# Six and five row buffers for gathered experts, and the low part of the weights last

## The chip, the cores and the metric

The kernel runs on one core of a Trainium2 chip. The metric is the device time of one execution in microseconds (us). Three runs of the kernel before gave 5113.34, 5116.54 and 5140.52 us; the median, 5116.54 us, is the number that the change is measured against.

The core has five engines that run their own instruction queues: TensorE (PE in the profile, with its weight loads as PEld), VectorE (DVE), ScalarE (ACT), GpSimd (POOL) and SyncE (SP, which here only issues DMAs). Each engine takes its instructions strictly in the order in which they were written out, so an instruction that waits holds up everything behind it on its engine.

## The reference

Two layers of a transformer-like trunk over 512 latent tokens and 256 context tokens of width 1024, float32. A layer is a mixer part (attention, pooling and a short convolution from one input projection, gated and projected back) and then an expert part:

```python
q = (xc @ w_q).reshape(PEER_CHUNK, PEER_HEADS, 2, PEER_HALF)
s = jnp.einsum('thid,hikd->thik', q, sub_keys)
...                                     # top 16 of 256 candidates a head: eidx, gate
u = u_emb[eidx]
hid = jax.nn.gelu(jnp.einsum('td,thkd->thk', xc, u))
wgt = gate * hid
return jnp.einsum('thk,thkd->td', wgt, v_emb[eidx])
```

There are 16384 experts, 8 heads and 16 experts a head, so each token uses 128 experts: 128 rows of `u_emb` and 128 rows of `v_emb`, of 1024 floats each. Layer 1 treats the latent tokens alone.

## The kernel before, in words

The expert part is computed in two ways at once.

**Dense.** For most latent tokens (512 in layer 0, 384 in layer 1) the kernel computes the first product for all 16384 experts, `hid = uT x y`, multiplies by a gate matrix that is zero almost everywhere, and multiplies by all of `v`. Experts come in 32 groups `c` of four tiles `e` of 128 experts. `hidden` does the first product: per tile it loads `uraw` (512 KB, SP queue), splits it into a high part `uh` (ScalarE) and a low part `ul` (VectorE, `ul = uraw - uh`), and issues 24 matmuls, three for each of eight blocks `k` of the contraction: `uh*yh`, `uh*yl`, `ul*yh`. These three stand together in `mm3` (lines 98, 99, 100). `uh` and `ul` have two buffers each, `hid` three accumulators in PSUM. `values` does the second product in the same manner: two groups at a time, four quarters `dq` of the output width; per quarter it loads and splits two tiles `vraw` into `vh` and `vl` and issues 48 matmuls into two accumulators `dps`. `weigh` makes the other operand, `wh` and `wl`, from the stored or kept `hid` and the gates `G`.

**Gathered.** The 256 context tokens of layer 0 and the last 128 latent tokens of layer 1 use their 128 experts only. `gathered` works on 128 tokens at a time, one token to a partition: `fetch` (line 854) issues an indirect DMA on GpSimd that brings one expert's row for each of the 128 tokens (128x1024 floats, 512 KB) into a buffer named `row`, and one VectorE instruction uses it: line 868 for a row of `u` (multiply and sum) and line 878 for a row of `v` (multiply and add into `gacc`). That is 256 fetches for 128 tokens, 512 in layer 0 and 256 in layer 1. `row` has three buffers, so a fetch waits until VectorE is done with the row three before it.

**The order of the work.** The kernel is written in a tile framework that plans the order of every engine's instructions with its own timeline and priorities (`prio`). The gathered work has the lowest priority (`late`, 40000), so the planner puts its instructions where it thinks VectorE is free; the loads and splits of the dense weights come early (`-ahead`). The planned order is then fixed: the engines do not change it at run time.

In layer 0 the gathered rows run beside the rest of the mixer (weights `wraw`, split into `whi` and `wlo`, products `mm`), the routing (`keys`, `pick`, `gates`), `hidden` and most of `values`. In layer 1 they run beside the routing, `hidden` and `values`. There, `experts` stores the first 20 groups of `hid` and keeps the last 12 in memory, so that `hidden` and `values` of those 12 alternate; in that part `vh` and `vl` have `EC + 2 = 4` buffers each (line 1139), and four in the part that follows (line 1146).

Of the kernel before, what the change touches and what calls it, by code (L numbers as in the profile page):

```python
# [21 lines left out]
F32 = mybir.dt.float32  # L22
# [10 lines left out]
P = 128  # L33
D = 1024
KT = D // P
# [34 lines left out]
class Net:  # L70
# [695 lines left out]
    def hidden(self, l, y, up, uq, cs, ahead, keep=False):  # L766

        nc, a = self.nc, self.a
        tiles = []
        for c in cs:  # L770
            if l:
                ge = up.tile([P, 4, y.n], F32, name="ge", bufs=1 + self.EC)
                tiles.append(ge)
            for e in range(4):
                with self.prio(-ahead):
                    raw = up.tile([P, KT, P], F32, name="uraw", bufs=3)
                    nc.sync.dma_start(raw.rearrange("p k e -> p (k e)"), a["uT"][l, 4 * c + e])
                    uh = up.tile([P, KT, P], F32R, name="uh", bufs=2)
                    ul = up.tile([P, KT, P], F32R, name="ul", bufs=2)
                    self.split(uh, ul, raw)  # L780
                hid = uq.tile([P, y.n], F32, name="hid", bufs=3)
                for k in range(KT):
                    self.mm3(hid, uh[:, k], ul[:, k], y.h[:, k], y.l[:, k], k == 0, k == KT - 1)
                with self.prio(-ahead):
                    g = ge[:, e] if l else up.tile([P, y.n], F32, name="ge", bufs=4)
                    nc.scalar.activation(g, hid, AF.Gelu_apprx_tanh)
                    if not l:
                        nc.scalar.dma_start(self.hidd[c][:, e * y.n:(e + 1) * y.n], g)
            if l and not keep:
                with self.prio(-ahead):  # L790
                    nc.scalar.dma_start(self.hidd[c][:, :4 * y.n], ge.rearrange("p e t -> p (e t)"))
        return tiles
# [56 lines left out]
    def gathered(self, l, tiles, gp, gq, nat, late):  # L849

        nc, a = self.nc, self.a

        def fetch(t, idx, s):
            r = gp.tile([P, D], F32, tag="row", name="row", bufs=3)
            nc.gpsimd.indirect_dma_start(out=r, out_offset=None, in_=a[t],  # L855
                                         in_offset=bass.IndirectOffsetOnAxis(ap=idx[:, s:s + 1], axis=0))
            return r

        for row, idx, g, hsrc, i, dst in tiles:
            with self.prio(late):  # L860
                x = gp.tile([P, D], F32, name="gx", bufs=1)
                nc.sync.dma_start(x, nat[row:row + P, :])
                acc = gp.tile([P, D], F32, name="gacc", bufs=1)
                for h in range(8):
                    hid = gp.tile([P, 16], F32, name="ghid", bufs=2)
                    for k in range(16):
                        r = fetch("peer_u", idx, h * 16 + k)
                        nc.vector.scalar_tensor_tensor(out=r, in0=r, scalar=1.0, in1=x, op0=OP.mult, op1=OP.mult,  # L868
                                                       accum_out=hid[:, k:k + 1])
                    w = gp.tile([P, 16], F32, name="gw", bufs=2)  # L870
                    nc.scalar.activation(w, hid, AF.Gelu_apprx_tanh)
                    nc.vector.tensor_tensor(w, w, g[:, h * 16:h * 16 + 16], op=OP.mult)
                    for k in range(16):
                        r = fetch("peer_v", idx, h * 16 + k)
                        if h == 0 and k == 0:
                            nc.vector.tensor_scalar(acc, r, w[:, k:k + 1], None, op0=OP.mult)
                        else:
                            nc.vector.scalar_tensor_tensor(acc, r, w[:, k:k + 1], acc, op0=OP.mult, op1=OP.add)  # L878
            res = gp.tile([P, KT, P], F32, tag="row", name="gres", bufs=3)
            nc.sync.dma_start(res, hsrc.rearrange("(k p) t -> p k t", p=P))  # L880
            tr = gq.tile([P, 4, P], F32, tag="gtr", name="gtr", bufs=1)
            for k in range(KT):
                nc.tensor.transpose(tr[:, k % 4], acc[:, k * P:(k + 1) * P], self.ident)
                nc.vector.scalar_tensor_tensor(res[:, k], tr[:, k % 4], self.modT[l][:, 40 + k, i:i + 1], res[:, k], op0=OP.mult, op1=OP.add)
            nc.sync.dma_start(dst.rearrange("(k p) t -> p k t", p=P), res)
# [10 lines left out]
    def run(self):  # L896
        nc, tc, a = self.nc, self.tc, self.a
        dt = lambda name, shape=(D, NT): tc.dram_tile(list(shape), F32, name=name)
        L = range(DEPTH)
        self.pd, self.od, self.md = [[dt(f"{n}{l}") for l in L] for n in ("pd", "od", "md")]  # L900
        self.qd, self.kd = [[dt(f"{n}{l}", (NH, P, 2, NT)) for l in L] for n in ("qd", "kd")]
        self.ld = [dt(f"ld{l}", (NH, P, NT)) for l in L]
        self.vd = [dt(f"vd{l}", (2, NH, P, NT)) for l in L]
        self.hmid = [dt(f"hmid{l}") for l in L]
        self.hout = dt("hout")
        self.natd = [dt("natd0", (NC, D)), dt("natd1", (P, D))]
        self.gd = dt("gd", (NX // 32, P, P * 32))
        self.hidd = dt("hidd", (32, P, 4 * NX))
        self.EC, self.stored = 2, 20
        X, Cx = Stream(0, NX, 0), Stream(NX, NC, 1)  # L910
        with ExitStack() as root:
            self.consts(self.pool(root, "consts"))
            ges = eh = h = None
            for l in L:
                ges, eh, h = self.trunk(l, X, Cx, ges, eh, h)
                ges, eh, h = self.ffn(l, ges, eh, h)
            eh.close()
            ges.close()
# [205 lines left out]
    def experts(self, l, y, up, uq, eu, e2):  # L1124


        n, EC, S = y.n, self.EC, self.stored
        with ExitStack() as es:
            self.hidden(l, y, up, uq, range(S), 12000)
            acc = self.pool(es, f"acc{l}").tile([P, KT, n], F32, name="acc")  # L1130
            va, vq = self.pool(es, f"va{l}"), self.pool(es, f"vq{l}", 1, PSUM)
            with ExitStack() as ev:
                vb = self.pool(ev, f"vb{l}")
                for c in range(S, 32 + EC, EC):
                    if c < 32:
                        ge = self.hidden(l, y, up, uq, range(c, c + EC), 0, True)
                    if c > S:
                        cs = range(c - EC, c)
                        self.values(l, n, cs, self.weigh(l, n, va, cs, had), lambda dq: (vb, 3, vb, EC + 2), vq, acc, c == S + EC)
                    had = ge  # L1140
                eu.close()
                e2.close()
            vb = self.pool(es, f"vc{l}", side="right")
            for c in range(0, S, EC):
                cs = range(c, c + EC)
                self.values(l, n, cs, self.weigh(l, n, va, cs), lambda dq: (vb, 3, vb, EC + 2), vq, acc, False,
                            vb if c == S - EC else None)
# [73 lines left out]
```

## Time and profile before

| | |
|---|---|
| median of three runs | 5116.54 us |
| profiled execution | 5126.48 us, span 5124.7 us |
| TensorE, busy share of the span | 95% |
| VectorE | 77% |
| ScalarE | 39% |
| GpSimd | 23% |
| DMA, mean | 250 GB/s |
| mean granted TensorE clock | 0.975 of full speed |

Busy TensorE is not TensorE at its peak: consecutive matmuls overlap, so the time of one matmul in the tables (its latency) is longer than the step from one to the next. The step is better read from a stretch that holds only matmuls of one kind, as the stretch divided by their count. A wait is the idle time of an engine before an instruction, put down to whatever released it last.

### The profile page before, as it was taken

Reading aid. Unit: us, or ns where it says so; the run is one execution under the profiler, and the core shown is the slowest. Engines: PE = TensorE matmul, PEld = TensorE weight load, DVE = VectorE, ACT = ScalarE, POOL = GpSimd, SP = SyncE. Lnnn points to the kernel's source line nnn. Section 1 sums busy time; section 2 is a strip of 40 time slices with the busy share of each in tenths; the row PEclk is TensorE's granted clock in tenths of the full one; section 3 lists DMA queues with packets and bytes.
Section 4 is the critical chain, followed back from the end, with each engine's and each line's share of the span. In section 5 each row is a group of like instructions: output and inputs, shape, how many; then the busy total and the mean of one; then the engine's idle time right before and its main releaser. Section 6 shows DMA issues by size and latency. Waiting matters only on the chain.

```text
span 5124.7 us, 74008 instructions
## 1 busy us (share of the span) xinstructions
PE 4846.5 (95%) x27373; PEld 4187.1 (82%) x27373; DVE 3946.3 (77%) x7996; ACT 1984.5 (39%) x2970; POOL 1199.9 (23%) x1060
## 2 busy tenths in 40 slices
PE   8999999798799999989999999999999999899999
PEld 5689787576588788768888879888679889899999
DVE  5468785977799998568888766777459999787885
ACT  4346665222233344323222334555334344332333
POOL 0012000144433343243334100100000433244320
PEclk9999999899899999999999999999899999999999
DMA  8668554488888888999999734543355888988995
GB/s 308 239 201 237 179 169 129 145 271 276 281 302 270 297 300 323 323 315 320 342 335 337 261 114 161 175 135 118 120 169 173 282 297 329 319 313 292 335 330 177
DMA packets 509419, 1280.77 MB, mean 250 GB/s; under 512 B 42880, under 2 KB 225024, under 8 KB 500736
## 3 DMA queue, kind: packets, MB, share of 16 engines
q1 hardware_dynamic: 302816, 669.35, 38.7%
q0 software_dynamic: 132352, 449.90, 26.1%
q10 hardware_dynamic: 73888, 156.79, 8.2%
q8 instruction: 215, 3.52, 0.3%
q14 instruction: 148, 1.21, 0.1%
HBM read 1098.13 MB, written 177.73 MB: 249 GB/s over the span
## 4 chain that ended last, share of the span: by engine, by line
PE 47%; DMA 14%; issue 11%; DVE 9%; POOL 3%; ACT 1%; POOLq 0%; DVEq 0%; ACTq 0%; SPq 0%
DMA row<-peer_v,ix 8%; PE dps L100 6%; PE dps L99 6%; PE dps L98 6%; DMA row<-peer_u,ix 5%; PE mm L98 4%; PE mm L100 4%; PE mm L99 4%; PE hid L100 4%; PE hid L98 4%; PE hid L99 3%; POOL row L855 3%; DVE gacc L878 2%; PE gps L760 1%; PE qk L100 1%
## 5 line engine op out<-in xcount | busy, mean ns | idle before, releaser
L100 PE MATMUL hid<-yh,ul 128*128 128x512 f32 (+1 forms) x2048 | 760.8, 373 | 55.3 <-DVE ul L94 54.9
L855 POOL DMA_INDIRECT row<-peer_v,ix x384 | 586.7, 1528 | 876.9 <-DVE gacc L878 537.4
L98 PE MATMUL hid<-yh,uh 128*128 128x512 f32 (+1 forms) x2048 | 758.3, 371 | 21.0 <-ACT yh L286 13.1
L855 POOL DMA_INDIRECT row<-peer_u,ix x384 | 503.5, 1311 | 1113.7 <-DVE row L868 614.3
L99 PE MATMUL hid<-yl,uh 128*128 128x512 f32 (+1 forms) x2048 | 755.9, 369 | 3.6 <-DVE yl L287 3.6
L100 PE MATMUL dps<-wh,vl 128*128 128x512 f32 (+1 forms) x2048 | 740.9, 364 | 11.8 <-DVE vl L94 11.8
L99 PE MATMUL dps<-wl,vh 128*128 128x512 f32 (+1 forms) x2048 | 741.1, 364 | 7.0 <-DVE wl L94 7.0
L98 PE MATMUL dps<-wh,vh 128*128 128x512 f32 (+1 forms) x2048 | 735.3, 364 | 8.9 <-ACT vh L93 8.9
L98 PE MATMUL mm<-hi,whi 128*128 128x512 f32 (+1 forms) x1856 | 665.5, 359 | 19.6 <-ACT rg L481 6.0
L100 PE MATMUL mm<-hi,wlo 128*128 128x512 f32 (+1 forms) x1856 | 658.6, 357 | 25.3 <-DVE wlo L94 25.0
L99 PE MATMUL mm<-lo,whi 128*128 128x512 f32 (+1 forms) x1856 | 659.8, 356 | 1.7 <-DVE lo L94 1.7
L878 DVE SCALAR_TENSOR_TENSOR gacc<-row,gw,gacc 128x1024 f32<-128x1024 f32 x381 | 488.2, 1281 | 166.9 <-DMA row<-peer_v,ix 165.4
L868 DVE SCALAR_TENSOR_TENSOR row<-row,gx 128x1024 f32<-128x1024 f32 x384 | 466.9, 1222 | 168.5 <-DMA row<-peer_u,ix 167.9
L94 DVE TENSOR_TENSOR wlo<-wraw,whi 128x1024 fp32r<-128x1024 f32 (+1 forms) x356 | 428.1, 1204 | 178.5 <-ACT whi L93 175.7
L93 ACT ACTIVATE uh<-uraw 128x1024 fp32r<-128x1024 f32 x256 | 271.3, 1060 | 689.5 <-PE hid L99 657.4
L93 ACT ACTIVATE whi<-wraw 128x1024 fp32r<-128x1024 f32 (+1 forms) x356 | 369.9, 1043 | 385.3 <-PE mm L99 270.1
L93 ACT ACTIVATE vh<-vraw 128x1024 fp32r<-128x1024 f32 x256 | 270.1, 1057 | 633.6 <-PE dps L99 387.9
L100 PEld LDWEIGHTS hid<-yh,ul 128*128 128x128 f32 x2048 | 391.2, 191 | 107.4 <-DVE ul L94 69.3
L98 PEld LDWEIGHTS hid<-yh,uh 128*128 128x128 f32 x2048 | 392.1, 192 | 63.6 <-ACT yh L286 14.7
L100 PEld LDWEIGHTS dps<-wh,vl 128*128 128x128 f32 x2048 | 386.3, 189 | 53.2 <-DVE vl L94 12.7
L99 PEld LDWEIGHTS hid<-yl,uh 128*128 128x128 f32 x2048 | 391.4, 191 | 44.7 <-DVE yl L287 5.0
L98 PEld LDWEIGHTS dps<-wh,vh 128*128 128x128 f32 x2048 | 386.6, 189 | 49.9 <-ACT vh L93 9.7
(337 smaller groups left out, 9481.1 us busy)
## 6 DMA issues: line engine op xcount, KB each, us to landing
uraw<-uT SPq DMA_DIRECT2D x256, 512.0 KB
vraw<-v SPq DMA_DIRECT2D x256, 512.0 KB
wraw<-w_in SPq DMA_DIRECT2D x216, 512.0 KB
gd<-gst ACTq DMA_DIRECT2D x28, 2048.0 KB
mw<-w_mod SPq DMA_DIRECT2D x96, 512.0 KB
wraw<-wq SPq DMA_DIRECT2D x80, 512.0 KB
hidd<-ge ACTq DMA_DIRECT2D x128, 256.0 KB
G<-gd SPq DMA_DIRECT2D x32, 1024.0 KB
```

The source lines that it names most:

```text
L93: self.nc.scalar.activation(hi, src, AF.Copy)
L94: self.nc.vector.tensor_tensor(lo, src, hi.bitcast(F32), op=OP.subtract)
L98: mm(ps, lh, rh, start=start, stop=False)
L99: mm(ps, lh, rl, start=False, stop=False)
L100: mm(ps, ll, rh, start=False, stop=stop)
L760: nc.tensor.matmul(ps[:, t], A[:, a_, :, t_], B[x][:, a_, :, t_], start=x == 0, stop=x == 1)
L855: nc.gpsimd.indirect_dma_start(out=r, out_offset=None, in_=a[t], in_offset=bass.IndirectOffsetOnAxis(ap=idx[:, s:s + 1], axis=0))
L868: nc.vector.scalar_tensor_tensor(out=r, in0=r, scalar=1.0, in1=x, op0=OP.mult, op1=OP.mult, accum_out=hid[:, k:k + 1])
L878: nc.vector.scalar_tensor_tensor(acc, r, w[:, k:k + 1], acc, op0=OP.mult, op1=OP.add)
```

## The change

Three edits. The row buffers become six in layer 0 and five in layer 1 (they were three). In layer 1, `vh` and `vl` have three buffers instead of four while `hidden` and `values` alternate; a buffer of `vh` and one of `vl` together are as large as the two more row buffers. And a tile of `hidden` issues its 16 matmuls with the high part `uh` first and its 8 matmuls with the low part `ul` behind them.

```diff
@@ hidden
                 hid = uq.tile([P, y.n], F32, name="hid", bufs=3)
+                mm = nc.tensor.matmul
                 for k in range(KT):
-                    self.mm3(hid, uh[:, k], ul[:, k], y.h[:, k], y.l[:, k], k == 0, k == KT - 1)
+                    mm(hid, uh[:, k], y.h[:, k], start=k == 0, stop=False)
+                    mm(hid, uh[:, k], y.l[:, k], start=False, stop=False)
+                for k in range(KT):
+                    mm(hid, ul[:, k], y.h[:, k], start=False, stop=k == KT - 1)
@@ gathered
-            r = gp.tile([P, D], F32, tag="row", name="row", bufs=3)
+            r = gp.tile([P, D], F32, tag="row", name="row", bufs=self.rows[l])
...
-            res = gp.tile([P, KT, P], F32, tag="row", name="gres", bufs=3)
+            res = gp.tile([P, KT, P], F32, tag="row", name="gres", bufs=self.rows[l])
@@ run
-        self.EC, self.stored = 2, 20
+        self.EC, self.stored, self.rows = 2, 20, (6, 5)
@@ experts
-                        self.values(l, n, cs, self.weigh(l, n, va, cs, had), lambda dq: (vb, 3, vb, EC + 2), vq, acc, c == S + EC)
+                        self.values(l, n, cs, self.weigh(l, n, va, cs, had), lambda dq: (vb, 3, vb, EC + 1), vq, acc, c == S + EC)
```

In the changed kernel the lines behind `hidden` have a number four higher: 855, 868 and 878 become 859, 872 and 882; the three matmuls of `hidden` stand in lines 784, 785 and 787. The planner makes a new order from these edits. Three places of it follow.

TensorE, layer 0, from one tile of `hidden` to the next, before (line 98 is `uh*yh`, 99 `uh*yl`, 100 `ul*yh`; the number of a name tells its buffer's use):

```order
L98 MATMUL hid_21152<-yh_14901,uh_21148 128x512
L99 MATMUL hid_21152<-yl_14902,uh_21148 128x512
L100 MATMUL hid_21152<-yh_14901,ul_21149 128x512
L98 MATMUL hid_21186<-yh_14901,uh_21182 128x512
L99 MATMUL hid_21186<-yl_14902,uh_21182 128x512
```

and the same turn from tile to tile in the changed kernel:

```order
L784 MATMUL hid_22444<-yh_14901,uh_22440 128x512
L785 MATMUL hid_22444<-yl_14902,uh_22440 128x512
L787 MATMUL hid_22444<-yh_14901,ul_22441 128x512 x8
L784 MATMUL hid_22478<-yh_14901,uh_22474 128x512
L785 MATMUL hid_22478<-yl_14902,uh_22474 128x512
```

Before, the low part was read by every third matmul, first by the third one; now all eight matmuls that read it stand at the end of the tile, and the first of them is the 17th.

GpSimd at the start of the gathered work of layer 0, before (`z` is a buffer of the convolution, of which GpSimd clears the two edges; rows of `peer_u` and `peer_v` are fetched 16 at a time):

```order
L855 DMA row<-peer_u,ix_11017 128x1024 x12
L573 MEMSET z 128x1
L574 MEMSET z 128x1
L573 MEMSET z 128x1
L574 MEMSET z 128x1
L855 DMA row<-peer_u,ix_11017 128x1024 x4
L855 DMA row<-peer_v,ix_11017 128x1024 x3
```

and now:

```order
L859 DMA row<-peer_u,ix_11017 128x1024 x16
L859 DMA row<-peer_v,ix_11017 128x1024 x5
L573 MEMSET z 128x1
L574 MEMSET z 128x1
L573 MEMSET z 128x1
L574 MEMSET z 128x1
L859 DMA row<-peer_v,ix_11017 128x1024 x4
```

Twelve fetches stood ahead of the first two buffers `z`, now 21.

VectorE in layer 1, while the gate matrix is made (`gA`, `gB`, `gE`) beside `hidden`, before (`gacc` uses a row of `v`):

```order
L94 TENSOR_TENSOR ul<-uraw,uh 128x1024
L752 TENSOR_TENSOR gB_40070<-gE,sl_35872 128x1024
L750 TENSOR_TENSOR gA<-iota_38404,sl_35870 128x1024
L753 TENSOR_TENSOR gB_40071<-gE,sl_35873 128x1024
L751 TENSOR_TENSOR gE<-iota_38404,sl_35871 128x1024
L878 SCALAR_TENSOR_TENSOR gacc<-row,gw,gacc 128x1024
L94 TENSOR_TENSOR ul<-uraw,uh 128x1024
```

and in the changed kernel (line 872 uses a row of `u`):

```order
L94 TENSOR_TENSOR ul<-uraw,uh 128x1024
L872 SCALAR_TENSOR_TENSOR row,ghid<-row,gx 128x1024
L752 TENSOR_TENSOR gB_39842<-gE,sl_35872 128x1024
L753 TENSOR_TENSOR gB_39843<-gE,sl_35873 128x1024
L872 SCALAR_TENSOR_TENSOR row,ghid<-row,gx 128x1024
L750 TENSOR_TENSOR gA<-iota_38404,sl_35870 128x1024
L872 SCALAR_TENSOR_TENSOR row,ghid<-row,gx 128x1024
L752 TENSOR_TENSOR gB_39870<-gE,sl_35872 128x1024
L753 TENSOR_TENSOR gB_39871<-gE,sl_35873 128x1024
L872 SCALAR_TENSOR_TENSOR row,ghid<-row,gx 128x1024
L751 TENSOR_TENSOR gE<-iota_38404,sl_35871 128x1024
L94 TENSOR_TENSOR ul<-uraw,uh 128x1024
```

One gathered row stood between two splits `ul` here, now four do. Over a whole layer the gathered rows stand closer together: counted in VectorE's order, the last of layer 0's 512 rows had 118 splits `vl` ahead of it and has 65 now, and the last of layer 1's 256 rows had 245 and has 209.

## Rows read from the trace of the kernel before

**Rows 1.** The page: busy us, share of the span and instructions of each engine.

```profile
PE 4846.5 (95%) x27373; PEld 4187.1 (82%) x27373; DVE 3946.3 (77%) x7996; ACT 1984.5 (39%) x2970; POOL 1199.9 (23%) x1060
```

**Rows 2.** Two slices of `values` alone: length, busy (count) by engine, clock, DMA.

```profile
2562.40:2690.50 128.10, 127.31 (x562) 105.09 (x562) 111.37 (x149) 35.39 (x45) 47.08 (x36) 1.00 0.97 335
...
4868.50:4996.60 128.10, 128.10 (x742) 127.92 (x742) 113.46 (x169) 46.99 (x65) 32.61 (x22) 1.00 0.95 330
```

**Rows 3.** TensorE's waits on splits: total, times, longest, in us.

```profile
PE hid L100 <- DVE ul L94: 54.9, 33, 5.8
PE mm L100 <- DVE wlo L94: 28.9, 16, 4.2
...
PE dps L100 <- DVE vl L94: 11.8, 2, 11.0
...
PE dps L98 <- ACT vh L93: 8.9, 2, 7.1
...
PE dps L99 <- DVE wl L94: 7.0, 5, 3.4
```

**Rows 4.** Waits around the gathered rows: who waited for whom.

```profile
POOL row L855 <- DVE row L868: 743.8, 273, 14.3
POOL row L855 <- DVE gacc L878: 660.8, 271, 15.0
...
DVE row L868 <- DMA row<-peer_u,ix: 167.9, 105, 7.6
DVE gacc L878 <- DMA row<-peer_v,ix: 165.4, 97, 6.4
```

**Rows 5.** GpSimd in order of time, `hidden` of layer 0: start, length, what, idle before.

```profile
2235.98 0.93 POOL L855 DMA_INDIRECT row<-peer_v,ix  x1 [2.99 <-DVE row L868]
2238.55 1.67 POOL L855 DMA_INDIRECT row<-peer_v,ix  x1 [1.64 <-DVE gacc L878]
```

**Rows 6.** VectorE in the same stretch.

```profile
2241.73 1.28 DVE L878 SCALAR_TENSOR_TENSOR gacc<-row,gw,gacc 128x1024 f32<-128x1024 f32 x1 [1.12 <-DMA row<-peer_v,ix]
2242.93 1.22 DVE L94 TENSOR_TENSOR ul<-uraw,uh 128x1024 fp32r<-128x1024 f32 x1
2247.23 2.61 DVE L878 SCALAR_TENSOR_TENSOR gacc<-row,gw,gacc 128x1024 f32<-128x1024 f32 x2 [3.08 <-DMA row<-peer_v,ix]
```

**Rows 7.** The costliest groups: count, busy us, mean ns, idle before.

```profile
L878 DVE SCALAR_TENSOR_TENSOR gacc<-row,gw,gacc 128x1024 f32<-128x1024 f32 x381 | 488.2, 1281 | 166.9 <-DMA row<-peer_v,ix 165.4
L868 DVE SCALAR_TENSOR_TENSOR row<-row,gx 128x1024 f32<-128x1024 f32 x384 | 466.9, 1222 | 168.5 <-DMA row<-peer_u,ix 167.9
...
L93 ACT ACTIVATE vh<-vraw 128x1024 fp32r<-128x1024 f32 x256 | 270.1, 1057 | 633.6 <-PE dps L99 387.9
```

**Rows 8.** Slices of 10 us around TensorE's longest wait for `ul`.

```profile
4390.00:4400.00 10.00, 6.63 (x39) 6.31 (x37) 1.23 (x2) 2.50 (x3) 1.36 (x2) 1.00 0.94 365
4400.00:4410.00 10.00, 7.56 (x30) 7.56 (x31) 4.81 (x7) 1.06 (x1) 2.61 (x2) 0.66 0.81 264
```

**Rows 9.** The stretches with gathered rows, whole and three parts.

```profile
1025.00:2947.00 1922.00, 1821.65 (x8988) 1496.75 (x8987) 1580.94 (x2774) 606.82 (x843) 704.48 (x520) 0.98 0.88 303
3972.00:4997.00 1025.00, 969.10 (x5962) 945.83 (x5961) 882.01 (x1477) 373.90 (x559) 375.75 (x257) 0.98 0.88 312
1025.00:1409.00 384.00, 326.71 (x1388) 257.96 (x1387) 287.50 (x403) 104.86 (x133) 164.90 (x142) 0.94 0.81 276
2306.00:2819.00 513.00, 509.80 (x2233) 420.99 (x2234) 444.30 (x600) 148.13 (x189) 186.98 (x137) 0.99 0.96 333
4484.00:4997.00 513.00, 495.86 (x2818) 492.20 (x2817) 430.04 (x597) 171.76 (x236) 193.42 (x141) 0.99 0.91 318
```

**Rows 10.** DMA issues of `values` in layer 0: count, KB each.

```profile
vraw<-v SPq DMA_DIRECT2D x256, 512.0 KB
...
G<-gd SPq DMA_DIRECT2D x32, 1024.0 KB
gel<-hidd SPq DMA_DIRECT2D x32, 1024.0 KB
```

## The prediction

> **What bounds the kernel now.** I read the page's busy times first. TensorE is busy for 95% of the span and no other engine for more than 77% [rows 1], so the end can only move if TensorE's idle time moves. Then its step: in two slices that hold almost nothing but `values`, 562 matmuls of 512 columns take 128.1 us and 742 of 384 columns the same, so a matmul costs 0.228 us and 0.173 us [rows 2]. A tile of `hidden` (24 matmuls) is then 5.5 us in layer 0 and 4.15 us in layer 1, and none of the edits changes a matmul's count or form. What can be won is waits.
>
> The list of TensorE's waits names who it waits for [rows 3]. The largest is the one for `ul`: 54.9 us in 33 waits. With `wlo` (28.9), `vl` (11.8) and `wl` (7.0) TensorE spends 102.6 us waiting for splits by VectorE. Why is VectorE late? It is not full. But it stands still 333 us for gathered rows that have not landed (167.9 and 165.4) [rows 4], and as it keeps its order, a split behind such a row is late too. GpSimd is not the cause: its fetches wait 1405 us (743.8 + 660.8) for VectorE to give a row buffer back. So the loop is: buffer given back, fetch, landing, use, three rows deep.
>
> How deep must it be? One stretch of `hidden` shows it. The fetch issued at 2235.98 is read by VectorE at 2241.73, after a wait, 5.75 us later; the next, issued at 2238.55, is read at 2247.23, 8.7 us later [rows 5, 6]. In `hidden` of layer 0 about two rows stand to a `ul`, so three rows back is 1.5 tiles, 8.2 us at TensorE's pace: no reserve against 5.75 to 8.7.
>
> **The change part by part.**
>
> *Low part last.* It removes nothing; it lets `ul` come 14 matmuls later (17th instead of third). That is 14 x 0.228 = 3.2 us in layer 0 and 14 x 0.173 = 2.4 us in layer 1. The mean of the 33 waits is 54.9 / 33 = 1.7 us, under both; the longest, 5.8 us, is over [rows 3]. At most 54.9 / 2.4 = 22 waits could be as long as the delay, in truth few are; I leave 10 us standing and take -45. The ends are -55 and 0 (0 if VectorE falls behind by so much more that the new slack is used up). `uh` is given back after 16 matmuls instead of 23, so ScalarE's split for the tile after next starts earlier; `ul` is given back at the end as before, and its split (1.22 us [rows 6]) then has 16 matmuls more before it is due. What is late next is `uh` itself, but ScalarE is busy for 39% only [rows 1].
>
> *Six and five row buffers.* Six rows back is three tiles, 16 us in the stretch above, against 5.75 to 8.7. Counting in the order all VectorE work that stands between a row's release and its next use, at the mean times of [rows 7] and of each other group, the median of that work grows from 7.4 to 13.1 us, and of 762 uses those with less than 7.3 us (the middle of 5.75 and 8.7) fall from 371 to 25. So most of the 333 us of VectorE's stalls should go as long as a fetch takes no longer than now. TensorE is paid only where a split stands behind: `wlo`, `vl`, `wl`, 47.7 us [rows 3] (the `ul` part is counted above). The ends are 0 and -48. I take -25, half: the same order also puts rows closer together, so part of the lead is spent.
>
> The Trainium skill (DMA: Bandwidth & Descriptors, section Anatomy of one DMA — SWDGE path) puts a GpSimd transfer at about 2.0 us plus its bytes over 436 GB/s; for a row fetch of 512 KB that is an estimate of 3.2 us. By that, three buffers would do already, this term would be 0 and the sum -31 instead of -56. The trace disagrees: 5.75 and 8.7 us from issue to use.
>
> *The clock.* Before TensorE's longest wait for `ul` the granted clock was 1.00 (2.4 GHz), in the 10 us after it 0.66, a mix of both levels, the lower being 1.2 GHz [rows 8]. The two stretches with gathered rows run at 0.98 on the mean [rows 9]: 2% of 2947 us, 59 us, is the most that lower clocks can take there, and most of it stands beside idle time that is counted already. With fewer waits I take -6; the ends are -20 and 0.
>
> *Three instead of four buffers of `vh` and `vl`.* It holds for 6 rounds of 4 quarters in layer 1. In a quarter two tiles are held, so one instead of two can be split ahead; the second waits until the first of the running quarter is done, and then takes a ScalarE and a VectorE split, 1.06 [rows 7] and 1.22 us. If nothing hid that: 24 x 2.3 = 55 us. But TensorE's new order there works through both accumulators' share of the first tile before it turns to the second, which gives the first tile back at half the quarter (24 x 0.173 = 4.2 us before its end), and `hidden` tiles stand between rounds. With four buffers the wait for `vh` was 8.9 us in 2 waits [rows 3]. Ends 0 and +55; I take +5. If that cover is gone, it shows as waits of `dps` for `vh`.
>
> *Denser rows.* The same 512 rows of layer 0 now end 118 - 65 = 53 splits `vl` earlier, 53 x 24 x 0.228 = 290 us of TensorE's pace; layer 1's end 36 earlier, 36 x 24 x 0.173 = 149 us. VectorE's work is only moved. But bytes must come faster. Layer 0: 1922 us x 303 GB/s = 582 MB [rows 9], less what `values` moves in those 53 tiles (0.52 MB of `vraw` and a quarter of `G` and `gel`, 0.5 MB, each [rows 10]: 54 MB), so 528 MB in 1632 us, 324 GB/s. Layer 1: 1025 x 312 = 320 MB, less 36 x 0.9 = 32 MB (`G` and `gel` are three quarters as large with 384 tokens), 288 MB in 876 us, 329 GB/s. The DMA engines gave 333 GB/s over 513 us while TensorE kept its step (2233 x 0.228 = 509 us) [rows 9]. So it fits, barely: on the mean no loss, but where the planner packs most tightly, at the start of the gathered work in the mixer (21 fetches instead of 12 ahead of the first `z`), the rate asked for is over it. I take +15; ends 0 and +58 (below).
>
> **The sum.** -45 - 25 - 6 + 5 + 15 = -56 us on the profiled execution of 5126.5 us, 5070 us. That execution lay 10 us above the median of the runs, so the same -56 on 5116.5 us: **5060 us**, 1.1% faster.
>
> **The rivals.**
>
> *Slower: the DMA engines become the bound.* Place: both stretches of [rows 9]. The point from which it decides is the rate: under 324 GB/s in layer 0 or 329 in layer 1 the rows land later than the new order assumes, VectorE stands still at them as before, and the splits behind are late again. If the rate stays at the 318 GB/s of layer 1's second half, layer 0 needs 528 / 0.318 = 1660 us (+28) and layer 1 288 / 0.318 = 906 us (+30): +58, 5175 us. For it: with `hidden` in the mix no long stretch got over 318. Against: 333 in `values`, 365 in a 10 us slice [rows 8], and the 0.81 share and 276 GB/s of the mixer stretch, where fetches were limited by depth and not by the engines. The Trainium skill (DMA: Bandwidth & Descriptors, section SWDGE vs HWDGE vs iDMA) says that a DMA engine takes turns between its queues; by that a GpSimd queue that never runs dry would take its turn from the weights' loads, and this rival would begin with late `uraw`. By that rule the time is this rival's; that TensorE kept its step at 333 GB/s [rows 9] speaks against it.
>
> *No change: the depth is spent.* The planner uses the buffers to pack rows tighter, so VectorE meets as many late rows as before; `ul` last still gives its 45 us, but term two is 0, tight packing costs 30 and `vh` 5: -10, 5106 us. For it: four rows between two `ul` where one stood. Against: the count of short leads, 371 to 25.
>
> *More: all split waits go.* -55 - 48 - 6 = -109, 5007 us; needs the 16 `wlo` waits of the mixer gone, where rows stand most tightly.
>
> **How the numbers follow.** Chances: forecast 0.55, all waits gone 0.10, no change 0.21, slower 0.14. A measurement of this kernel can tell 0.5%, 26 us, from no change, so faster means under 5091 us and slower over 5142 us. The first two cases are faster (0.65), the third the same. The range is 5005 to 5140: below it half of the second case is left out, above it the slower one, together about 0.19.
>
> **What would show it.** Right: `hid` waits for `ul` near 10 us; VectorE's waits for rows well under 333 us; the gathered rows of layer 0 end near 2600 us; DMA at 320 GB/s or more in both stretches. Wrong: VectorE's waits for rows still near 300 us at a DMA share over 0.95 (slower rival); waits of `dps` for `vh` or `vl` of 20 us or more between 4350 and 4750 us (the smaller `vh` pool); waits of ScalarE's splits `uh` and `whi` for their loads.

## The result, and the profile after

The changed kernel takes 5038.77 us (median of four runs, 5036.24 to 5048.67), against 5114.94 us for the kernel before on the same chip: a ratio of 0.9843, 95% interval 0.9809 to 0.9877, 1.6% faster. The forecast was 5060 us. The profiled execution took 5040.68 us with a span of 5038.9 us, 85.8 us less than the span before.

TensorE's busy time is nearly the old one over a shorter span [rows 1]. The page's first part, then its DMA rows over 40 slices of 126 us:

```profile
PE 4813.7 (96%) x27373; PEld 4175.7 (83%) x27373; DVE 3948.5 (78%) x7996; ACT 2016.5 (40%) x2970; POOL 1208.6 (24%) x1060
...
DMA  8668564399998889999965534543355998999865
GB/s 304 238 202 237 170 187 132 103 352 353 368 336 298 313 326 355 367 353 354 359 204 188 174 128 156 175 137 110 121 176 176 335 334 332 352 335 331 302 221 174
```

Slices 9 to 20 hold layer 0's gathered rows, 32 to 38 layer 1's. In twelve of those nineteen slices the DMA engines give 335 GB/s or more; the prediction's slower rival had them stay at 318.

The longest of TensorE's waits after, where [rows 3] stood (total, times, longest, in us):

```profile
PE dps L98 <- ACT vh L93: 35.6, 5, 31.5
...
PE hid L784 <- ACT yh L286: 17.4, 3, 10.8
...
PE hid L784 <- ACT uh L93: 12.0, 5, 4.9
...
PE dps L100 <- DVE vl L94: 8.4, 7, 2.9
...
PE hid L787 <- DVE ul L94: 2.5, 4, 1.8
...
PE mm L100 <- DVE wlo L94: 0.5, 1, 0.5
```

The wait for `ul` at line 787 is down to 2.5 us in 4 waits, all in layer 1; the one for `wlo` is down to 0.5 us. The largest is now one for `vh`, of 31.5 us.

The gathered rows themselves, where [rows 4] and [rows 7] stood: who waited, then VectorE's two groups with the idle time before them.

```profile
POOL row L859 <- DVE gacc L882: 487.6, 227, 15.1
POOL row L859 <- DVE row L872: 422.2, 189, 16.8
...
DVE row L872 <- DMA row<-peer_u,ix: 18.7, 23, 2.2
...
DVE gacc L882 <- DMA row<-peer_v,ix: 8.2, 4, 5.8
```

```profile
L882 DVE SCALAR_TENSOR_TENSOR gacc<-row,gw,gacc 128x1024 f32<-128x1024 f32 x381 | 486.7, 1277 | 10.9 <-DMA row<-peer_v,ix 8.2
L872 DVE SCALAR_TENSOR_TENSOR row<-row,gx 128x1024 f32<-128x1024 f32 x384 | 461.7, 1217 | 19.1 <-DMA row<-peer_u,ix 18.7 <-issue 0.4
```

VectorE stood still 333 us for rows and does so for 27 now, at the same length of each instruction.

Where the 85.8 us came from is read best in stretches that hold the same work. I cut both traces at the first matmul of `hidden` and the first of `values` in each layer; the counts of matmuls then agree to about 1%. Before (length, busy time and count by engine, clock, DMA share, GB/s):

```profile
1025.00:1361.00 336.00, 286.81 (x1158) 222.87 (x1156) 247.63 (x318) 85.22 (x107) 145.32 (x132) 0.95 0.82 277
1361.00:2286.00 925.00, 891.51 (x5012) 744.45 (x5013) 783.88 (x1720) 331.48 (x495) 338.38 (x232) 0.98 0.87 301
3803.00:4420.00 617.00, 575.20 (x3961) 554.29 (x3961) 551.28 (x1428) 255.57 (x406) 168.18 (x105) 0.97 0.76 270
4420.00:5120.00 700.00, 682.01 (x3870) 677.73 (x3871) 554.40 (x782) 234.54 (x323) 207.57 (x152) 0.99 0.85 293
```

and the same work after:

```profile
1025.00:1311.00 286.00, 272.04 (x1170) 220.50 (x1170) 270.10 (x347) 87.76 (x108) 178.29 (x145) 0.98 0.96 357
1311.00:2214.00 903.00, 883.33 (x5012) 741.83 (x5012) 829.39 (x1786) 344.98 (x495) 387.56 (x277) 0.99 0.92 335
3743.00:4360.00 617.00, 565.73 (x3961) 549.22 (x3961) 580.10 (x1467) 265.42 (x404) 217.13 (x134) 0.95 0.81 296
4360.00:5034.00 674.00, 672.95 (x3868) 671.90 (x3869) 526.19 (x742) 238.21 (x323) 177.25 (x123) 1.00 0.81 280
```

The mixer of layer 0 gives 50 us of the 86, `hidden` of layer 0 22, layer 1 26 (all in its `values`); the rest of layer 0 takes 12 us more. Of the mixer's 50, TensorE's waits make 39 (all of them together were 42.5 us before and are 3.9 now). The clock makes about 11, an estimate from the two rows: at 0.95 of full speed 336 us lose 17, at 0.98 286 us lose 6.

What TensorE waited for there, before, in 1025 to 1361:

```profile
PE mm L100 <- DVE wlo L94: 23.4, 13, 4.2
PE nps L275 <- DVE hmid L631: 8.7, 1, 8.7
PE mm L98 <- DVE cg L616: 3.6, 3, 1.8
```

Besides `wlo`, two more results of VectorE (`hmid`, `cg`) stood behind stalled rows.

### The profile page after: what moved, and what is told of

It reads as the page before. It is cut to its first block, busy times and chain, and to the rows that moved or that the text cites. A ratio compares the mean times of both kernels' runs of the same rounds, so it can differ in the third digit from the quotient of the medians.

```text
span 5038.9 us, 73941 instructions
## 1 busy us (share of the span) xinstructions
PE 4813.7 (96%) x27373; PEld 4175.7 (83%) x27373; DVE 3948.5 (78%) x7996; ACT 2016.5 (40%) x2970; POOL 1208.6 (24%) x1060
## 3 DMA queue, kind: packets, MB, share of 16 engines
q0 software_dynamic: 132352, 449.90, 25.4%
## 4 chain that ended last, share of the span: by engine, by line
PE 68%; DVE 8%; issue 5%; DMA 4%; ACT 2%; POOL 1%; SPq 0%; ACTq 0%; DVEq 0%; POOLq 0%
PE dps L100 7%; PE dps L98 7%; PE hid L784 7%; PE dps L99 7%; PE hid L785 7%; PE hid L787 7%; PE mm L98 5%; PE mm L99 5%; PE mm L100 5%; PE gps L760 2%; DVE row L872 1%; PE qk L100 1%; PE qk L98 1%; PE qk L99 1%; DMA vraw<-v 1%
## 5 line engine op out<-in xcount | busy, mean ns | idle before, releaser
L859 POOL DMA_INDIRECT row<-peer_u,ix x384 | 517.7, 1348 | 750.6 <-DVE row L872 280.3
L787 PE MATMUL hid<-yh,ul 128*128 128x512 f32 (+1 forms) x2048 | 470.1, 366 | 2.6 <-DVE ul L94 2.5
L99 PEld LDWEIGHTS dps<-wl,vh 128*128 128x128 f32 x2048 | 386.1, 189 | 42.4 <-DVE wl L94 2.1
L98 PEld LDWEIGHTS mm<-hi,whi 128*128 128x128 f32 x1856 | 357.2, 192 | 69.4 <-ACT rg L481 7.6
```

Of the source, the lines that this page charges most:

```text
L98: mm(ps, lh, rh, start=start, stop=False)
L99: mm(ps, lh, rl, start=False, stop=False)
L787: mm(hid, ul[:, k], y.h[:, k], start=False, stop=k == KT - 1)
```

## The experiments

All were timed beside the kernel before, whose median was 5125.26 us for E1 to E4, 5116.89 for E5 to E8 and 5121.52 for E9 to E12. The table gives the ratio to it with its 95% interval, and, from the one profiled execution of each, how long the stages took (us): up to the first `hidden` of layer 0, that `hidden`, from `values` to the first `hidden` of layer 1, then layer 1's `hidden` and `values` (to its last matmul). E8 is the changed kernel once more, and its stages lie within 3 us of the first time. Every edited kernel has a plan of its own, so the depth of the buffers and the order of the work always change together.

| | ratio | mixer | hidden 0 | values 0 to hidden 1 | hidden 1 | values 1 |
|---|---|---|---|---|---|---|
| before | 1 | 1362 | 924 | 1518 | 616 | 700 |
| after | 0.9843 [0.9809, 0.9877] | 1311 | 903 | 1529 | 617 | 674 |
| E1 low part last alone | 1.0003 [0.9991, 1.0015] | 1371 | 928 | 1510 | 599 | 705 |
| E2 all but low part last | 0.9865 [0.9846, 0.9884] | 1307 | 906 | 1527 | 618 | 684 |
| E3 rows (6, 3) | 0.9853 [0.9837, 0.9869] | 1323 | 902 | 1517 | 598 | 701 |
| E4 E1 + small `vh`, `vl` | 0.9986 [0.9974, 0.9999] | 1368 | 938 | 1517 | 600 | 701 |
| E5 rows after gate block 8 | 0.9837 [0.9816, 0.9859] | 1318 | 903 | 1518 | 547 | 747 |
| E6 rows after block 12 | 0.9841 [0.9816, 0.9866] | 1310 | 903 | 1523 | 516 | 771 |
| E7 rows (4, 3) | 0.9843 [0.9820, 0.9865] | 1330 | 892 | 1508 | 599 | 707 |
| E8 the change again | 0.9837 [0.9815, 0.9860] | 1310 | 902 | 1526 | 618 | 675 |
| E9 E6, half arithmetic | 0.9814 [0.9799, 0.9829] | 1304 | 901 | 1528 | 516 | 766 |
| E10 E6, half bytes | 0.9746 [0.9730, 0.9762] | 1308 | 905 | 1524 | 520 | 726 |
| E11 rows (4, 3), no low part last | 0.9897 [0.9880, 0.9914] | 1331 | 898 | 1509 | 622 | 705 |
| E12 rows after block 4 | 0.9840 [0.9824, 0.9855] | 1308 | 901 | 1529 | 534 | 756 |

**E1, the low part last alone.** From the changed kernel:

```diff
-        self.EC, self.stored, self.rows = 2, 20, (6, 5)
+        self.EC, self.stored, self.rows = 2, 20, (3, 3)
...
-    ... lambda dq: (vb, 3, vb, EC + 1), vq, acc, c == S + EC)
+    ... lambda dq: (vb, 3, vb, EC + 2), vq, acc, c == S + EC)
```

> The low part last alone: three row buffers in both layers and four buffers of vh and vl, as before. My theory (TensorE waits for splits that stand behind late rows on VectorE; the later use of ul rides the stalls out): waits of hid for ul fall from 54.9 to under 15 us, VectorE's waits for rows stay at 280 to 360 us, the waits of mm for wlo stay near 29 us, and the time falls by 30 to 55 us, to 5060 to 5085. Rival (the row buffers do all, low last is superfluous beside them): at most 15 us faster.

Measured: 5125.87 us, no change: the gain that I expected is missing and the rival holds. Its waits:

```profile
DVE row L872 <- DMA row<-peer_u,ix: 187.8, 108, 9.4
DVE gacc L882 <- DMA row<-peer_v,ix: 142.4, 97, 5.3
PE mm L100 <- DVE wlo L94: 26.4, 19, 3.5
PE dps L98 <- ACT vh L93: 25.4, 2, 23.6
PE hid L787 <- DVE ul L94: 20.7, 16, 4.3
```

The wait for `ul` fell by 34 us, as the edit should do, and the end did not move. In `hidden` of layer 0 it fell from 16.8 to 6.1 us, but TensorE waited 41.1 us there in all (39.9 before), now for `keys`, `gA` and `gtr`, and VectorE stood still for rows 110 us instead of 87. In layer 1 the wait for `ul` in `hidden` fell from 24.4 to 3.0 us and the stage became 17 us shorter, although it ends in a wait of 23.6 us for `vh` (7.1 before); the mixer, which the edit does not touch but the planner's order does, became 9 us longer and `values` 5. The stage behind `hidden` of layer 0 became 8 shorter, but this execution also lay 8 us under the median of its runs.

**E2, the row buffers (and three buffers of `vh` and `vl`) alone.**

```diff
-                mm = nc.tensor.matmul
                 for k in range(KT):
-                    mm(hid, uh[:, k], y.h[:, k], start=k == 0, stop=False)
-                    mm(hid, uh[:, k], y.l[:, k], start=False, stop=False)
-                for k in range(KT):
-                    mm(hid, ul[:, k], y.h[:, k], start=False, stop=k == KT - 1)
+                    self.mm3(hid, uh[:, k], ul[:, k], y.h[:, k], y.l[:, k], k == 0, k == KT - 1)
```

> Six and five row buffers and three buffers of vh and vl, but the three matmuls of hidden side by side as before. My theory: VectorE's waits for rows fall to under 60 us, and with them the waits for wlo and most of those for ul (under 20 us); the time falls by 40 to 75 us, to 5040 to 5075, so the two edits together give less than the sum of each alone. Rival (both are needed, ul waits have causes of their own): ul waits stay over 35 us and the time falls by 20 to 35 us only.

Measured: 5053.59 us, 0.9865, so 69 us of 5125 without the low part last, as the theory had it. Its waits:

```profile
PE dps L98 <- ACT vh L93: 36.2, 6, 29.0
DVE row L868 <- DMA row<-peer_u,ix: 18.3, 21, 2.4
PE hid L100 <- DVE ul L94: 16.0, 19, 2.6
```

TensorE's wait for `ul` fell from 54.9 to 16.0 us with the matmuls in their old order: most of it was a late row one step removed, and the deeper buffers cure it at its source.

**E3, six buffers in layer 0 only** (`self.rows = 2, 20, (6, 3)` in that line of E1, with its four `vh` and `vl`).

> Low part last in both layers, six row buffers in layer 0, but three in layer 1 and four buffers of vh and vl. The changed kernel has a new hole in layer 1: dps waits 31.5 us for vh behind the last gates. Theory that the denser rows of layer 1 fill VectorE while the gates are made and so delay the gates: the hole is gone or under 8 us, and the time is 5010 to 5040. Rival that the hole comes with the dense part (low part last, hid ahead of the gates): it stays at 20 us or more, and the time is 5040 to 5070.

Measured: 5046.94 us, 0.9853, within the interval of the whole change: the rival's time, and the theory that the denser rows of layer 1 make the gap missed. Layer 1's five buffers are worth nothing that can be told; with four buffers of `vh` and `vl` TensorE still waits 27.1 us for `vh`, once for 23.5.

**E4, E1 with the smaller `vh` and `vl`** (only the first line of E1's diff).

> Low part last with three row buffers in both layers, and three instead of four buffers of vh and vl in layer 1: against the low part last alone this is the price of the smaller pool. My theory: 0 to 12 us more than low last alone, with waits of dps for vh and vl under 20 us between 4350 and 4750 us. Rival: the smaller pool makes the hole of the changed kernel; a wait of dps for vh of 20 us or more and 25 us or more in the time.

Measured: 5119.72 us, 0.9986. The wait for `vh` is 24.8 us (25.4 in E1), over the 20 that I expected at most, but it does not come from the smaller pool, which costs nothing that can be told. So the 31.5 us have another cause. The trace of the changed kernel shows it (start, length, instruction, idle before; ACTq and SPq are the engines' DMA issues):

```profile
4329.34 0.33 ACTq L763 DMA_DIRECT2D gd<-gst  x1
...
4339.02 2.93 SPq L805 DMA_DIRECT2D G<-gd  x2
4342.04 8.85 SPq L830 DMA_DIRECT2D vraw<-v  x3
...
4359.06 1.06 ACT L93 ACTIVATE vh<-vraw 128x1024 fp32r<-128x1024 f32 x1 [7.24 <-DMA vraw<-v]
...
4360.16 0.69 PE L98 MATMUL dps<-wh,vh 128*128 128x384 f32 x1 [31.49 <-ACT vh L93]
```

`G` reads what the last gate store wrote, and `vraw` stands behind `G` on SP's queue: the first `dps` stands 31 us behind that store (23 to 32 us in the seven other runs whose rows of layer 1 start at once, E8 among them). When the store comes is set by VectorE, which makes the gates between gathered rows and in the changed kernel is busy without a break just before it:

```profile
4265.00:4325.00 60.00, 47.48 (x362) 43.44 (x361) 59.96 (x90) 22.91 (x37) 30.01 (x19) 0.86 0.95 360
```

Before, the last gate store was at 4389 us and the first `dps` at 4420, also 31 us later, but TensorE still had `hidden` to do in those 31 us (first row, before; then the changed kernel):

```profile
4389.00:4420.00 31.00, 18.23 (x90) 17.59 (x89) 15.92 (x26) 8.19 (x13) 7.91 (x7) 0.85 0.93 338
```

```profile
4329.00:4360.00 31.00, 0.00 (x0) 0.00 (x0) 17.55 (x22) 3.18 (x6) 12.43 (x11) 0.50 1.03 372
```

What TensorE wins ahead of the store it waits for behind it.

**E5 and E6, layer 1's rows held back** until the 8th or the last of its 12 gate blocks, by making the index depend on that block's gates:

```diff
...
+                        st = self.gates(l, mp, pp, sl, 4 * t + b, iota2, self.gd)
+                        if l and 4 * (nd - 1 - t) + b + 1 == 8:      # 12 in E6, 4 in E12
+                            ix, go = self.held
+                            zero = self.small1.tile([P, 1], F32, name="zero")
+                            nc.vector.tensor_scalar(zero, st[:, 0, 0:1], 0.0, None, op0=OP.mult)
+                            nc.vector.tensor_scalar(ix, ix, zero, None, op0=OP.add)
+                            go()
...
```

> The changed kernel, but in layer 1 the gathered rows may start only when 8 of the 12 gate blocks are made (the indices are made to wait for the eighth). Theory: in layer 1 the start of values is pinned to the last store of gates (first dps 31 us after it both before and in the changed kernel), and the rows fill VectorE, which makes the gates, so the gates end late and time that TensorE wins ahead of them is paid back there. Then the last gate store moves from 4329 to under 4290 us, the wait of dps for vh falls from 31.5 to under 10 us, and the time is 4990 to 5020 us. Rival (the gates hang on their own chain and on the dense splits, not on the rows): the last store stays over 4310 us, the wait over 20 us, and the time is 5030 to 5060.

> As the run before, but the rows of layer 1 start only behind all 12 gate blocks. Theory: the gates end at least as early (last store under 4280 us) and the wait of dps for vh is under 10 us, but 256 rows now share the rest of layer 1 with hidden and values: time 4990 to 5030, and the last row is read after 4850 us. Rival as before; a second rival is that the rows end so late that the end waits for them: then gacc or the last transposes stand on the chain at the end and the time is over 5040.

Measured: 5039.37 and 5035.89 us, both the time of the change and not the gain that I expected. The rows do hold up the gates: the last gate store came at 4200 and 4188 us instead of 4329, and the gap went (longest wait for `vh` 2.1 and 2.8 us; first `dps` at 4286 and 4251 us instead of 4360). But `values` became longer by as much. In E6, from the first `dps` to 50 us behind the last row (4940 us), and to the last `dps`:

```profile
4250.00:4990.00 740.00, 712.86 (x4020) 700.86 (x4021) 655.86 (x903) 257.51 (x349) 314.96 (x233) 0.99 0.95 337
4251.00:5022.00 771.00, 744.86 (x4204) 732.86 (x4205) 671.63 (x926) 262.94 (x354) 314.96 (x233) 0.99 0.93 328
```

Two engines are nearly full there, the DMA engines (0.95) and VectorE (655.86 of 740 us), and TensorE waits. E9 and E10 tell the two apart.

**E7, four buffers in layer 0, three in layer 1** (`(4, 3)` in E1's line, with its four `vh` and `vl`).

> Low part last, four row buffers in layer 0, three in layer 1, four buffers of vh and vl: beside the run with six and three this is one point of the series over depth (three: 5125, six: 5047). My theory (what counts is the lead against a landing of 6 to 9 us; four rows back are about 11 us in hidden, less in the mixer): VectorE's waits for rows of both layers, 330 us with three and 98 us with six and three, become 150 to 230 us, and the time 5065 to 5095. Rival (any depth over three lets the planner pack as tightly, and the gain is the new plan's): within 10 us of the run with six, 5040 to 5057. Second rival (the rate of the DMA engines is what counts, depth matters little below six): over 5105.

Measured: 5041.15 us, 0.9843: all of the gain, with one row buffer more in layer 0 and the low part last. My theory (5065 to 5095 us) missed; the time is the one of the rival that any depth over three will do. Its reason does not hold, though: the plan does not pack the rows as tightly as with six, since the last row of layer 0 has 100 splits `vl` ahead of it (118 before, 65 in the change) and is read at 2692 us. VectorE still stands still 150 us for rows, in the whole run and then in layer 1 alone:

```profile
DVE row L872 <- DMA row<-peer_u,ix: 85.2, 63, 8.1
DVE gacc L882 <- DMA row<-peer_v,ix: 64.8, 55, 3.8
...
PE mm L100 <- DVE wlo L94: 10.0, 8, 2.5
PE hid L787 <- DVE ul L94: 7.2, 5, 3.1
```

```profile
DVE row L872 <- DMA row<-peer_u,ix: 51.9, 31, 8.1
DVE gacc L882 <- DMA row<-peer_v,ix: 36.9, 30, 3.8
```

So 89 of the 150 us are layer 1's, which has three buffers as before (102 us there before). In layer 0 the fourth buffer cuts the stall from 231 to 61 us, and the mixer gets its bytes faster (277 GB/s before, 357 in the change):

```profile
1025.00:1330.00 305.00, 277.16 (x1168) 221.23 (x1168) 262.39 (x334) 87.01 (x108) 162.29 (x140) 0.97 0.92 325
```

Against E3, which differs from it in layer 0's depth alone, the stages show where six are no better: they win 7 us in the mixer and lose 10 in `hidden` and 9 behind it (why was not pursued).

**E8, the change again** beside E5 to E7.

> The changed kernel once more, beside the runs above and with more rounds, to put low last in the company of the deeper rows against the rows alone (ratio 0.9865 to before). My theory: the low part last gives 0 to 15 us there: ratio 0.983 to 0.9865. Rival (it costs): ratio over 0.988.

Measured: 5038.57 us, 0.9837. Against E2 (0.9865, timed in another set) the low part last is worth 0.0028, 14 us, on top of six and five buffers, but the intervals overlap, so that it is worth anything there is not shown.

**E9, half of layer 1's gathered arithmetic left out**, on E6:

```diff
+        W = D // 2 if l else D
-    ...scalar_tensor_tensor(out=r, in0=r, scalar=1.0, in1=x, ...
+    ...scalar_tensor_tensor(out=r[:, :W], in0=r[:, :W], scalar=1.0, in1=x[:, :W], ...
-    ...scalar_tensor_tensor(acc, r, w[:, k:k + 1], acc, ...
+    ...scalar_tensor_tensor(acc[:, :W], r[:, :W], w[:, k:k + 1], acc[:, :W], ...
```

> The kernel whose rows of layer 1 start after the 12th gate block, and of each of those 256 rows VectorE uses only the first 512 of 1024 floats (half of the gathered arithmetic of layer 1 is left out; every byte is still fetched). It asks what holds layer 1 once the gap before its `values` is gone: there the time won up to 4497 us was given back behind it. If VectorE is what is short, 256 x about 0.6 us = 150 us of its work go, its busy share in 4250 to 4997 falls from 0.88 to about 0.7, and the time falls by 20 to 45 us against the same kernel with whole arithmetic (ratio to before 0.975 to 0.980). If the DMA engines are short (share 0.92 to 0.97 there), at most 5 us are gained (0.983 to 0.985) and VectorE's waits for rows grow instead.

**E10, half of layer 1's gathered bytes left out**, on E6:

```diff
-            r = gp.tile([P, D], F32, tag="row", name="row", bufs=self.rows[l])
-            nc.gpsimd.indirect_dma_start(out=r, out_offset=None, in_=a[t],
+            r = gp.tile([P, W], F32, tag="row", name="row", bufs=self.rows[l])
+            nc.gpsimd.indirect_dma_start(out=r, out_offset=None, in_=a[t].rearrange("r (h c) -> (r h) c", h=2) if l else a[t],
...
+                            r = r[:, None, :].to_broadcast([P, 2, D // 2])
```

> The same kernel, rows of layer 1 after the 12th gate block, with the other half left out: each fetch of layer 1 brings 512 floats of another row (256 KB instead of 512 KB) and VectorE reads them twice, so its work stays as long and the DMA engines move 256 x 0.25 MB = 67 MB less. If the DMA engines are short, the share in 4250 to 4997 falls from 0.95 to about 0.75 and the time by 20 to 45 us (ratio to before 0.975 to 0.980). If VectorE is short, at most 5 us are gained (0.983 to 0.985), with VectorE busy for 88% of that stretch as before and TensorE waiting for `vl` and `uh` as before.

Measured: E9 5025.47 us (0.9814), E10 4990.84 us (0.9746). Against E6 (0.9841, timed in another set) half the arithmetic gives 0.0027, 14 us, less than a shortage of VectorE was to give and more than the 5 of its rival, with intervals that overlap (VectorE's waits for rows, which were to grow, are 28.6 us against 24.7); half the bytes gives 0.0095, 49 us, a little over what a shortage of the DMA engines was to give. The same stretch in E9 and E10:

```profile
4249.00:5015.00 766.00, 740.08 (x4205) 732.44 (x4206) 553.45 (x926) 262.45 (x354) 267.25 (x233) 0.99 0.92 331
```

```profile
4257.00:4983.00 726.00, 723.08 (x4161) 719.94 (x4160) 656.31 (x915) 256.16 (x348) 324.00 (x227) 1.00 0.78 258
```

In E9 VectorE's work falls by 118 us against E6's 671.63, and the stage by 5 of 771 us. In E10 VectorE is as full as in E6, the DMA share is 0.78, and the stage is 45 us shorter. So `values` of layer 1 beside gathered rows is short of bytes in E6; the changed kernel itself was not run with half of them. It shows as ScalarE's wait for `vraw` from 3972 to 4997 us, in E6 and then in E10:

```profile
ACT vh L93 <- DMA vraw<-v: 124.2, 39, 11.3
```

```profile
ACT vh L93 <- DMA vraw<-v: 57.3, 15, 9.3
```

The Trainium skill (DMA: Bandwidth & Descriptors, section Queues, rings and completion order) says that each DMA engine serves its queues in turn, a packet at a time; that dense loads come earlier when the rows are halved agrees with it, though no run here separates turns from a plain lack of bandwidth.

**E11, four buffers in layer 0 without the low part last** (E7 with the `hidden` of E2).

> Four row buffers in layer 0 and nothing else: the low part's matmuls stand beside the others, layer 1 keeps three row buffers and four of `vh` and `vl`. The same with the low part last gave 5041 us (0.9843). If one more row buffer is the whole of the change's gain, this gives 0.984 to 0.989 (5035 to 5061 us), with waits of `hid` for `ul` of 10 to 25 us. The rival: at four buffers VectorE still stands still 150 us for rows, so `ul` is late more often and the low part last is needed: 0.990 or more, waits for `ul` over 35 us.

Measured: 5069.28 us, 0.9897. It lies between the theory (up to 0.989) and the rival (0.990 or more), the wait for `ul` on the rival's side:

```profile
PE hid L100 <- DVE ul L94: 36.4, 26, 4.4
```

One more buffer alone gives 53 us of 5121.5; with it the low part last is worth 0.9897 - 0.9843 = 0.0054, 28 us, as much as the wait for `ul` falls (36.4 to 7.2). E7 was timed in another set, but the intervals do not overlap.

**E12, layer 1's rows after the 4th gate block** (the diff of E5 with 4).

> The changed kernel with the rows of layer 1 held until the 4th of the 12 gate blocks is stored, between starting at once (gap of 31 us before `values`, 0.9837) and after the 8th (gap of 2 us, time paid back at the end, 0.9837). If both losses are of VectorE's work having no room, it is moved again: 0.982 to 0.985. The rival: a middle start keeps the gap short and leaves the end free, 0.980 or less (5012 us), the last row before 4800 us and waits of `dps` for `vh` under 10 us.

Measured: 5036.86 us, 0.9840. The gap is gone (longest wait for `vh` 3.5 us, first `dps` at 4272) and the time is the same again: the rival's 5012 us is out. No version beats the changed kernel by what can be measured.

## Why the prediction was right, and where it was not

The sum, -56 us, came out at -76 in the runs' medians and inside the range, by the mechanism that was named for the row buffers (rows back sooner, VectorE's stalls gone, splits on time). That the sum lies so near is in part luck: its largest term gives nothing by itself and the next is almost three times too small, and these two errors largely cancel.

**Low part last, -45.** The step that failed is the count of the 54.9 us as the order's own. What the edit does to its wait was right (20.7 us left in E1, 2.5 in the change). But alone it gives 0 (E1), with four row buffers 28 (E11 against E7), with six and five 14, with intervals that overlap (E2 against E8). The step took a wait that goes for time that is won. With three buffers VectorE is as late as before, and in `hidden` of layer 0 TensorE waited for other results instead, 41.1 us against 39.9. In layer 1's `hidden`, of 21 us of waits for `ul`, 16 came back as the longer wait for `vh`; the 17 us by which the stage is shorter all the same were lost in the mixer (9), in layer 0's `hidden` (4) and in layer 1's `values` (5). This is not the case given as the lower end, in which `ul` itself would have stayed late.

**Row buffers, -25.** Measured 69 (E2). Two things were wrong. The same late rows stood behind most of the waits for `ul`, so the two edits are cures for one wait and their terms do not add: -45 and -25 were split by the name of the wait, where the cause was shared. And in the mixer I took half of the waits for `wlo`; all of them went, with those for `hmid` and `cg` that I had not counted, and the lower clock beside them.

**Clock, -6.** In the mixer alone about -11; in layer 1's `hidden` it fell from 0.97 to 0.95, in the stretch that ends with the gap. That is inside the ends of -20 and 0.

**`vh` and `vl`, +5.** Nothing that can be told in E4. The mark that I set for it, waits of `dps` for `vh` of 20 us or more, did appear, but for another reason: it is in E1, E3 and E11 (21.4 us) with four buffers too. It marks the gate store, and I had not looked for what pins the start of `values`.

**Denser rows, +15.** In the mixer, where I put the cost, there is none. The rate I feared was 324 GB/s; the mixer got 357, since three buffers, not the engines, had held it at 277. What denser rows cost behind it was not measured by itself; six buffers lose 19 us against four there (E3 against E7). In layer 1 the engines do bind in E6 (E10), but as a ceiling on the gain and not as a loss against the kernel before: there the time won by closing the gap (E5, E6, E12) is not kept. That five buffers give nothing there (E3) for the same reason is likely and not shown. The slower rival thus had the right resource in one layer and the wrong consequence. The count of 256 `vraw` in [rows 10] is that of both layers; layer 0 has 128, four to a `G`, as the sum takes it.

The four signs of being right held: VectorE's stalls are far under 333 us, the wait for `ul` is under the 10 us that I left standing, the 512th row of layer 0 is read at 2523 us (2600 forecast), and the rate is over 320 GB/s in both layers from the first row to the last:

```profile
1025.00:2523.00 1498.00, 1445.48 (x7410) 1195.75 (x7411) 1379.53 (x2506) 517.81 (x712) 690.45 (x516) 0.98 0.95 344
3909.00:4728.00 819.00, 767.12 (x4881) 751.16 (x4880) 759.71 (x1276) 316.49 (x464) 388.74 (x253) 0.97 0.93 338
```

Of the signs of being wrong, two appeared: the wait for `vh`, and ScalarE's waits of `uh` for its load, 3.7 us before and 53.1 now:

```profile
ACT uh L93 <- DMA uraw<-uT: 53.1, 31, 4.0
```

It is 50.3 us in E1 and 14.6 in E2, so most of it comes with the low part last, which gives `uh` back earlier, and not with the denser rows. Little of it reaches TensorE, whose wait for `uh` went from 7.4 to 12.0 us.

The estimate of 3.2 us for a row's transfer by the Trainium skill (DMA: Bandwidth & Descriptors, section Anatomy of one DMA — SWDGE path), which would have made three buffers enough, is contradicted by the result and by E7's list of DMA issues, where the median from issue to landing is 7.4 us:

```profile
row<-peer_u,ix POOLq DMA_INDIRECT x384, 7.4
```

What stays open: why the planner's order with the low part last alone makes the mixer 6 to 9 us longer (E1, E4); the stages come from one profiled execution each, and this was not pursued. And no run holds the order of the work fixed while the depth changes, so how much of the gain is the depth's own and how much the new order's is not shown; what is shown is that VectorE's stalls in layer 0 (231, 61 and 10 us with three, four and six buffers) and TensorE's waits for splits go down together.

## What to carry to other kernels

Two waits behind one late engine are one cost: before adding the terms of two edits, ask whether either alone would remove both, and run each alone. When an in-order engine stalls on a low-priority stream, deepen that stream's buffers by one first and measure; here the fourth buffer in one layer gave 53 us and six and five buffers 69, and with the low part last both gave the same. Where closing a visible gap does not move the end, halve the bytes and the arithmetic of the stage separately to see which one gives the time back.

## What the runs showed of the hardware

The 16 DMA engines gave 357 GB/s over the 286 us of the mixer at a share of 0.96, and up to 368 over a whole slice of 126 us, with 512 KB row fetches and 512 KB weight loads mixed; in the kernel before the same mixer ran at 277 GB/s and 0.82, with four buffers (E7) at 325 and 0.92: it looked far from a limit because its fetches waited for buffers.
